# One load for the single-row B tiles of two batches, and a first load of 64 two-row descriptors, in a batched trace of a matrix product

## Chip, cores and metric

One core of a Trainium2 chip. The time is the device time of one execution in microseconds (us), as the median of several executions; lower is better. Engines go by their names in the profile: PE is TensorE, DVE is VectorE, ACT is ScalarE, POOL is GpSimd, SP is the sync engine. A descriptor orders one piece of a transfer and shows as one packet in the DMA records. A completion is the 4-byte packet with which each of the 16 DMA engines ends a load.

## The reference, cut to what matters

```python
B, N = 8, 2176
a, b: float32 [8, 2176, 2176]
prod = np.matmul(a, b)
traces = np.diagonal(prod, axis1=1, axis2=2).sum(axis=-1)     # float32 [8]
```

The trace of A·B needs no product: it is the sum over all elements of A transposed times B. The kernel has to read both inputs once, 303 MB of float32.

## The kernel before

A is loaded with a cast to bfloat16, transposed on TensorE and copied from PSUM into `at`; B is loaded with the same cast; DVE multiplies the two and sums. The loads go out from GpSimd, in one order. Per batch, A comes in groups of 6, 6 and 5 rows per partition, B in groups of 6, 6, 4 and 1. This is about the group with 1 and about the very first load, which must not wait for GpSimd and is therefore issued on the sync engine, without a cast.

```python
even = [6, 6, 4, 1]
UNEVEN = ((0, 64), (64, 116), (116, 123), (123, P))
...
single = ctx.enter_context(tc.tile_pool(name="single", bufs=3))
...
def fetch(t, src, start, m, parts=((0, P),)):
    rows = src[start:start + P * m, :].rearrange("(p r) k -> p r k", r=m)
    for lo, hi in parts:                       # usually one part, all 128 partitions
        with in_order():
            issued = nc.gpsimd.dma_start(out=t[lo:hi], in_=rows[lo:hi])
        loaded.append(issued)
    return t
...
def load_first(src, start):                    # 128 rows of A, one per partition
    words = stage.tile([P, MOST, N], bf16, tag="stage")
    plain = words.bitcast(f32).rearrange("p r k -> p (r k)")[:, :N]
    half = N // 2
    t = single.tile([P, 1, N], bf16, tag="single")
    nc.sync.dma_start(out=plain, in_=src[start:start + P, :])
    nc.scalar.copy(out=t[:, 0, :half], in_=plain[:, :half])
    nc.vector.tensor_copy(out=t[:, 0, half:], in_=plain[:, half:])
    return t
...
if not last:
    for start, m in b_groups:
        parts = UNEVEN if bi == BATCH // 2 and m == 1 else ((0, P),)
        on_dve(start // P, load(b[bi], start, m, parts))
```

`UNEVEN` cuts one single-row load into pieces whose sizes are no multiples of 16, so that the 16 DMA engines get different amounts. That is a means to balance them. The transposes of the first group and the end of the last batch are in the whole kernel.

## Time and profile before

| | before |
|---|---|
| median time | 709.01 us (708.89 to 709.24, 6 runs) |
| span of the profiled run | 707.4 us |
| share of the 16 DMA engines' span on GpSimd's queue | 99.8% |

The page and the chain are read in the prediction below. Three lines of the timeline at the start and one at the end are wanted later. The columns are start, duration, engine, line, operation, tiles; in brackets the idle time before and what ended it (SPq is the sync engine's issue of a DMA).

```profile
0.74 0.40 SPq L90 DMA_DIRECT2D words<-in_a_dram  x1
...
5.89 1.10 ACT L91 CAST t<-words 128x1088 bf16<-128x1088 f32 x1 [3.87 <-DMA words<-in_a_dram]
5.89 0.73 DVE L92 CAST t<-words 128x1088 bf16<-128x1088 f32 x1 [5.02 <-DMA words<-in_a_dram]
...
703.97 0.42 DVE L125 CUSTOM_DVE_ANT_0 at<-at,b_t 128x256 bf16<-128x256 bf16 x1 [0.24 <-DMA b_t<-in_b_dram]
```

The first load is used at 5.89 us, and the last piece of B at 703.97 us.

### The profile page before, as it was taken

The page shows a single profiled execution, that of the slowest core. Times are in us where ns is not written, and L with a number is a line of the kernel's source. Part 1 is how long each engine was busy: PE and PEld are TensorE (multiplying, and loading weights), DVE is VectorE, ACT ScalarE, POOL GpSimd, SP SyncE. Part 2 cuts the span into 40 slices and gives each one's busy share as a digit, 9 for nine tenths or more (in the row PEclk, how much of TensorE's full clock was granted, in tenths as well). Part 3 has the DMA queues.
Part 4 walks back from the last instruction along what each step waited for, and adds up shares of the span by engine and source line. Part 5 has one row for each costly group of instructions (what it writes and reads, how often), then busy time and mean ns, then how long its engine had stood idle before and what let it go on. Part 6 is the DMA issues. An engine that isn't in the chain of part 4 may idle for free.

```text
span 707.4 us, 3226 instructions
## 1 busy us (share of the span) xinstructions
PE 206.9 (29%) x1313; PEld 191.4 (27%) x1313; DVE 390.4 (55%) x132; ACT 202.8 (29%) x165; POOL 35.1 (5%) x72
## 2 busy tenths in 40 slices
PE   2452005700067000670016600156002660025504
PEld 1452005600066000560016500156002550025403
DVE  0216981359813597235972369623696227962397
ACT  2363005710057100570005800057001570016600
POOL 1000000000000000000000100000000000000200
PEclk9766556865567655785557955588555685557855
DMA  9999999999999999999999999999999999999997
GB/s 232 217 212 214 208 231 206 217 230 199 221 222 217 216 223 214 215 218 218 214 214 214 222 217 217 214 217 220 214 220 216 217 220 215 213 217 215 214 217 154
DMA packets 9025, 152.29 MB, mean 215 GB/s; under 512 B 1074, under 2 KB 1330, under 8 KB 2610
## 3 DMA queue, kind: packets, MB, share of 16 engines
q0 software_dynamic: 8864, 150.97, 99.8%
q1 hardware_dynamic: 146, 1.11, 0.5%
q8 instruction: 10, 0.16, 0.1%
q14 instruction: 5, 0.04, 0.0%
HBM read 303.04 MB, written 0.00 MB: 428 GB/s over the span
## 4 chain that ended last, share of the span: by engine, by line
DMA 56%; another core or an unknown queue 22%; issue 9%; PE 6%; ACT 3%; DVE 3%; POOL 1%; POOLq 0%; DVEq 0%; ACTq 0%
DMA t<-in_a_dram 30%; DMA t<-in_b_dram 21%; PE ps L148 6%; DMA b_t<-in_b_dram 5%; ACT at L120 3%; DVE at L125 2%; DVE at L118 1%; PE ps L172 0%; POOL t L73 0%; POOL b_t L255 0%; POOL shared L73 0%; POOL identity masks.py:199 0%; POOL identity masks.py:197 0%; DVE diagonal L125 0%
## 5 line engine op out<-in xcount | busy, mean ns | idle before, releaser
L120 ACT COPY at<-ps 128x1536 bf16<-128x1536 bf16 (+6 forms) x163 | 200.4, 1311 | 461.7 <-PE ps L148 445.5
L148 PE MATMUL ps<-identity,t 128*128 128x128 f32 x1071 | 187.4, 346 | 464.9 <-DMA t<-in_a_dram 443.5
L125 DVE CUSTOM_DVE_ANT_0 at<-at,t 128x13056 bf16<-128x13056 bf16 (+2 forms) x28 | 273.1, 9790 | 59.1 <-DMA t<-in_b_dram 59.1
L148 PEld LDWEIGHTS ps<-identity,t 128*128 128x128 f32 x1071 | 174.9, 212 | 476.5 <-issue 446.9
L118 DVE COPY at<-ps 128x1536 bf16<-128x1536 bf16 (+4 forms) x54 | 85.1, 1575 | 242.5 <-PE ps L148 213.0
L125 DVE CUSTOM_DVE_ANT_0 at<-at,shared 128x8704 bf16<-128x8704 bf16 (+3 forms) x5 | 29.2, 5838 | 5.8 <-DMA shared<-in_b_dram 5.8
L73 POOL DMA_DIRECT2D t<-in_b_dram x31 | 16.3, 531 | 264.9 <-PE ps L172 209.8
L73 POOL DMA_DIRECT2D t<-in_a_dram x24 | 13.0, 540 | 322.7 <-DVE sums L125 246.9
L265 PEld LDWEIGHTS <-at 128*128 128x128 bf16 x68 | 6.4, 132 | 30.6 <-issue 30.1
L172 PE MATMUL ps<-identity,t 128*128 128x128 bf16 x170 | 13.8, 219 | 2.9 <-ACT at L120 2.4
L265 PE MATMUL trace_ps<-shared,at 128*128 128x128 bf16 x59 | 5.9, 284 | 28.7 <-DMA shared<-in_b_dram 28.7
L172 PEld LDWEIGHTS <-t 128*128 128x128 bf16 x170 | 11.8, 99 | 5.4 <-issue 5.3
L73 POOL DMA_DIRECT2D shared<-in_b_dram x6 | 3.2, 532 | 47.3 <-PE ps L172 38.7
L92 DVE CAST t<-words 128x1088 bf16<-128x1088 f32 x1 | 0.7, 728 | 5.0 <-DMA words<-in_a_dram 5.0
L125 DVE DVE_READ_ACCUMULATOR2_ANT sums<- 128x1 f32 x28 | 2.3, 83 | 0.0
L91 ACT CAST t<-words 128x1088 bf16<-128x1088 f32 x1 | 1.1, 1098 | 3.9 <-DMA words<-in_a_dram 3.9
L265 PE MATMUL trace_ps<-b_t,at 128*128 128x128 bf16 x9 | 1.4, 296 | 1.1 <-DMA b_t<-in_b_dram 1.1
L255 POOL DMA_DIRECT2D b_t<-in_b_dram x3 | 1.6, 546 | 0.9 <-DMA shared<-in_b_dram 0.9
L125 DVE CUSTOM_DVE_ANT_0 at<-at,b_t 128x256 bf16<-128x256 bf16 (+1 forms) x3 | 1.5, 514 | 0.3 <-DMA b_t<-in_b_dram 0.2
L91 ACT ACT_TABLE_LOAD x1 | 1.3, 1283 | 0.7 <-PEq L307 0.7
L125 DVE DVE_READ_ACCUMULATOR2_ANT late<- 128x1 f32 x9 | 0.7, 82 | 0.0
L273 DVE TENSOR_REDUCE result<-total 1x7 f32<-1x28 f32 x1 | 0.2, 174 | 1.0 <-PE total L272 1.0
(13 smaller groups left out, 2.5 us busy)
## 6 DMA issues: line engine op xcount, KB each, us to landing
t<-in_a_dram POOLq DMA_DIRECT2D x16, 3264.0 KB, 45.1
t<-in_b_dram POOLq DMA_DIRECT2D x14, 3264.0 KB, 49.0
t<-in_a_dram POOLq DMA_DIRECT2D x7, 2720.0 KB, 42.4
t<-in_b_dram POOLq DMA_DIRECT2D x7, 2176.0 KB, 44.0
shared<-in_b_dram POOLq DMA_DIRECT2D x3, 2176.0 KB, 38.9
t<-in_b_dram POOLq DMA_DIRECT2D x6, 544.0 KB, 46.0
t<-in_a_dram POOLq DMA_DIRECT2D x1, 2176.0 KB, 14.9
words<-in_a_dram SPq DMA_DIRECT2D x1, 1088.0 KB, 5.1
```

The costliest lines, as they stand in the source:

```text
L73: issued = nc.gpsimd.dma_start(out=t[lo:hi], in_=rows[lo:hi])
L91: nc.scalar.copy(out=t[:, 0, :half], in_=plain[:, :half])
L92: nc.vector.tensor_copy(out=t[:, 0, half:], in_=plain[:, half:])
L118: last_copy = nc.vector.tensor_copy(out=dst, in_=src)
L120: nc.scalar.copy(out=dst, in_=src)
L125: nc.vector.tensor_tensor_reduce(out=x if out is None else out, in0=x, in1=y, scale=1.0, scalar=0.0, op0=MUL, op1=ADD, accum_out=acc,)
L148: nc.tensor.transpose(ps[:, n * m + r, :], words[:, r, c0:c0 + step * (P - 1) + 1:step], tiles[f32],)
L172: last_transpose = nc.tensor.transpose(ps16[:, n, r, :], a_t[:, r, c0:c0 + P], tiles[bf16],)
L255: loaded.append(nc.gpsimd.dma_start(out=row[:, lo:hi], in_=b[bi, start:start + P, lo:hi]))
L265: nc.tensor.matmul(trace_ps, x, y, start=(n == 0), stop=(n == len(pe_work) - 1),)
L273: nc.vector.reduce_sum(out=result[:1, 0:done], in_=total[:, 0:early].rearrange("o (b n) -> o b n", n=per_batch), axis=mybir.AxisListType.X,)
```

## The change

The intent is to save descriptors and completions in a kernel that only the DMA engines hold up: three loads for six single-row tiles of B, and 64 descriptors of two neighbouring rows (17,408 bytes) for the first load where there were 128 of one. The pieces move to the pair of batches 2 and 3. The diff, cut to its core (left out: the transposes for a tile with 64 partitions, and the renaming that splits `fetch` from the row pattern):

```diff
-    UNEVEN = ((0, 64), (64, 116), (116, 123), (123, P))
+    UNEVEN = ((0, 96), (96, 122), (122, P))
+    UNEVEN_BATCH = 2
...
-    single = ctx.enter_context(tc.tile_pool(name="single", bufs=3))
+    single = ctx.enter_context(tc.tile_pool(name="single", bufs=1))
+    pair_pool = ctx.enter_context(tc.tile_pool(name="pair", bufs=1))
...
-        plain = words.bitcast(f32).rearrange("p r k -> p (r k)")[:, :N]
-        t = single.tile([P, 1, N], bf16, tag="single")
-        nc.sync.dma_start(out=plain, in_=src[start:start + P, :])
-        nc.scalar.copy(out=t[:, 0, :half], in_=plain[:, :half])
-        nc.vector.tensor_copy(out=t[:, 0, half:], in_=plain[:, half:])
+        plain = words.bitcast(f32).rearrange("p r k -> p (r k)")[:, :2 * N]
+        t = pair_pool.tile([P, 2, N], bf16, tag="pair")
+        flat = t.rearrange("p r k -> p (r k)")
+        nc.sync.dma_start(
+            out=plain[32:96, :], in_=src[start:start + P, :].rearrange("(p r) k -> p (r k)", r=2)
+        )
+        nc.scalar.copy(out=flat[0:32, :], in_=plain[32:64, :])
+        nc.vector.tensor_copy(out=flat[32:64, :], in_=plain[64:96, :])
+        return t[0:64]
...
-                parts = UNEVEN if bi == BATCH // 2 and m == 1 else ((0, P),)
-                on_dve(start // P, load(b[bi], start, m, parts))
+                if m > 1 or bi == BATCH - 2:
+                    on_dve(start // P, load(b[bi], start, m))
+                    continue
+                if bi % 2 == 0:
+                    pair = pair_pool.tile([P, 2, N], bf16, tag="pair")
+                    both = b[bi:bi + 2, start:start + P, :].rearrange("b p k -> p b k")
+                    fetch(pair, both, UNEVEN if bi == UNEVEN_BATCH else ((0, P),))
+                on_dve(start // P, pair[:, bi % 2:bi % 2 + 1, :])
```

## The prediction

> **What bounds the kernel now.** I read the engine table and the slices of the page first, because they say which resource is never idle.
>
> ```profile
> PE 206.9 (29%) x1313; PEld 191.4 (27%) x1313; DVE 390.4 (55%) x132; ACT 202.8 (29%) x165; POOL 35.1 (5%) x72
> ...
> DMA  9999999999999999999999999999999999999997
> ```
>
> No compute engine is busy over 55% of the span, while the DMA row is 9 in every slice but the last. The queue part of the page says whose work that is.
>
> ```profile
> DMA packets 9025, 152.29 MB, mean 215 GB/s; under 512 B 1074, under 2 KB 1330, under 8 KB 2610
> q0 software_dynamic: 8864, 150.97, 99.8%
> q1 hardware_dynamic: 146, 1.11, 0.5%
> ...
> HBM read 303.04 MB, written 0.00 MB: 428 GB/s over the span
> ```
>
> The queue that GpSimd fills (loads with a cast from f32 to bf16) occupies the 16 DMA engines for 99.8% of the span. Only the first load, which has no cast, is on q1. Next, the chain of work in order of time, for the depth of the queue:
>
> ```profile
> 78.72 14.17 issue
> 92.89 0.01 POOLq L73
> 92.91 42.48 DMA t<-in_a_dram
> ...
> 670.56 33.38 DMA b_t<-in_b_dram
> 703.95 0.02 issue
> 703.97 0.42 DVE at L125
> ```
>
> A load issued at 92.91 us lands 42.48 us later, although its own data needs only some 13 to 15 us. The rest, about 28 us, is the wait behind earlier loads. So an issue that comes a few us late costs nothing. At the other end only 1.3 us of work (705.25 less 703.95) follow the last landing.
>
> The DMA records of the trace give the cost model. A 26,112-byte packet lasts 1942 ns, one of 17,408 bytes 1302 ns, one of 4352 bytes 342 ns; sizes are counted on the written side. All fit bytes / 13.6 B per ns plus 22 ns. Packets of one engine overlap by about 18 ns, so the start-to-start distance is bytes / 13.6 plus about 3.5 ns. A completion packet between two transfers adds about 21 ns. Per whole load with 6 rows this gives 8 x 1923.5 + 21 = 15,409 ns; completions of successive such loads stand 15,408 ns apart. The model is exact enough to count nanoseconds.
>
> **What the Trainium skill says.** All four are in "DMA: Bandwidth & Descriptors". (1) Section "Where 436 GB/s comes from" gives a port ceiling of 435.2 GB/s for the 16 engines. Our 13.6 B/ns written is 27.2 B/ns read, or 435 GB/s over 16 engines, and 428 GB/s are seen over the span. So the transfers are at the ceiling, and only overhead and unevenness remain. (2) Section "Why a DMA increments its semaphore by 16 and not by 1": some direct copies through GpSimd put ceil(partitions / 16) partitions on each engine in turn. The trace agrees: in the four-part load of batch 4, packet counts per engine are 10 on five engines, 9 on two, 8 on six, 4 on three. That is 4 each, plus 4 on engines 0 to 12 (52 partitions), plus 1 on engines 0 to 6 (7), plus 1 on engines 0 to 4 (5). The numbers 0 to 15 are my reading by that rule; the trace shows the counts. (3) Section "The descriptor swizzle": four neighbouring partitions belong to one engine, with a step from one half of the engines to the other at partition 64. Partitions 32 to 95 then give each engine four partitions, hence 4 packets of 17,408 bytes. No run so far shows this. (4) Section "Queues, rings and completion order" has an engine drain a packet of several descriptors from one ring before it changes rings. This agrees with the start: on each engine the first GpSimd packet begins only after the 8 packets of the first load (earliest completion 5.007 us, next packet 5.013 us).
>
> **The change, part by part.**
>
> *B tiles with one row, batches 0 to 5.* Removed: six loads of 544 KB, of which the one of batch 4 was in four pieces. Added: three loads of 1088 KB, of which the one of batches 2 and 3 is in three pieces. Batch 6 keeps a load of its own. The bytes are the same. The source rows of two batches are far apart, and the built instruction has the shape 128 x 2 x 2176, so I expect 256 packets of 4352 bytes per whole pair: no fewer packets. Completions: before, six whole singles (6 x 21 = 126 ns) and some 91 ns for the four pieces (a 9-packet engine took 3002 ns where 9 x 323.5 is 2911), in all 217 ns. After: two whole pairs and one single (63 ns) and three pieces, about 70 ns: 133 ns. Saving 0.08 us on every engine. Should the packets become 8704 bytes, 24 packets per engine fall away, and 24 x 3.5 = 0.08 us more.
>
> *First load.* Same 1.11 MB, at 8704 B in 328 ns per packet; 4 packets of 640 + 4 instead of 8 of 320 + 4 save 0.015 us of pure transfer. The beginning is less sure. The engines start between 1.76 and 2.65 us, most first packets last about 1 us (up to 1.43) and nearly all end near 3.0 to 3.3. Half as many descriptors might bring the late starters forward. I put 0.1 to 0.2 us on that.
>
> *Casts of the first load.* Each now has 32 partitions x 4352 elements instead of 128 x 1088. ACT took 1.10 us for 1088, so about 4.4 us for four times the length; DVE 0.73 us, so about 2.9 us. They end near 10 us instead of 7. Then come 16 f32 and 2 bf16 transposes with 64 rows and nine small copies, some 4 us, before the next A tile lands (its transposes began at 16.16 us). The B load that waits for this buffer is issued near 10 us instead of 7.28, and it lies behind loads that run until 46 us. Off the path: 0.
>
> *Buffers.* Single tiles go from three buffers to one, with one pair buffer beside it. The pair of batches 2 and 3 must wait for DVE's last product of batch 1; in the queue it stands behind all six other loads of batch 2, several of which need buffers freed no earlier. Batch 7's pieces wait for batch 6's product, near 630 us, and were issued at 668.6. Off the path: 0. Odd batches have one load less, so the 28 us of depth varies by 2.6 us (8 x 323.5), far from empty.
>
> *Balance of the engines.* The end is the slowest engine, not the mean. Ten instruction fetches of 16 KB (892 to 975 ns each) put whichever engine they fall on about 1.1 us behind. Comparing the 16 completion times of each load, I get the lag against the earliest engine near the end: 0, 1043, then thirteen between 1193 and 2351, and 2542 ns for the last. Mean about 1860, so the last engine is 0.68 us past it. The new pieces 96, 26 and 6, two rows each, put 18 packets on engines 0 to 5, 16 on 6 to 12, 12 on 13 to 15, where even is 16. Before, against an even 8: +2 on engines 0 to 4, +1 on 5 and 6, 0 on 7 to 12, -4 on 13 to 15. The only difference is engine 5 (+1, or 323 ns later) and engine 6 (-1, 323 ns earlier). Those two now hold the lags 2236 and 2542. If 6 is the later one, the maximum goes from 2542 to about 2560; if 5 is, to about 2865. So 0 to +0.32 us, with the start offsets (0 to 0.53 us) reshuffled by the new first load on top. I take +0.05, since whoever changed the pieces probably moved work the right way.
>
> Sum: -0.08 - 0.015 - 0.15 + 0.05 = -0.2 us, and with half a chance of merged packets -0.04 more: about -0.25 us.
>
> **The rivals.** First, balance dominates: a different first load and fetches falling elsewhere could put a lagging engine on +2 packets and the end 0.3 to 0.6 us later, 709.3 to 709.6. The 1.1 us per fetch speaks for it; against it, the pieces are nearly the same as before. Second, the queue runs dry: the pair buffer or the late casts delay an issue so far that DMA idles. It would cost whole microseconds, 711 or more, but 28 us of depth against a 3 us delay speaks against it. Third, the two-run pattern moves slower than one run. Half the rate on the three pairs, 3 x 5.2 us of transfer, would add up to 15 us and give 724; but rows of 8704 source bytes already moved at the ceiling as singles. Fourth, a better balance than I can work out: at most the 0.68 us above the mean, which gives about 708.
>
> **Range and chances.** From 709.0 us less 0.25 I predict 708.7 us. The range 707.9 to 709.4 covers a balance gain of most of the 0.68 us with the start's 0.2, and the bad balance of the first rival. 2% are 14 us; there is nothing of that size outside the third rival, so within 2% has 0.98.
>
> **What would show it.** DMA stays at 9 in all slices and GpSimd's queue near 99.8%; 256 packets per pair show as unchanged counts of 4352-byte packets (1152), a smaller count as merging. The first GpSimd packet starts near 4.9 us instead of 5.01. The first casts take about 4.4 and 2.9 us and nothing at 16 us moves. The completions of the last load show the balance. Wrong would be: a 0 to 8 in the DMA row, DVE or PE waiting on a load of pairs for many us, or a pair that takes clearly more than 5.2 us of the queue.

## The result, and the profile after

The changed kernel takes 709.37 us (median of 6 runs, 709.32 to 709.47) beside 709.01 us. The ratio is 1.0005, with a 95% interval from 0.9992 to 1.0018. It is the mean time of the one kernel's runs over that of the other's from the same rounds, so not quite the ratio of these medians. Its interval holds 1. Yet the lowest of the six is above the highest of the six before, so I take the 0.36 us as real and look for it. 708.7 was predicted, with a range to 709.4: inside, at the edge, and with the wrong sign.

From the page of the changed kernel, the DMA row of the slices and the queues:

```profile
DMA  9999999999999999999999999999999999999997
...
DMA packets 8897, 152.29 MB, mean 215 GB/s; under 512 B 1010, under 2 KB 1266, under 8 KB 2546
...
q0 software_dynamic: 8800, 150.97, 99.8%
q1 hardware_dynamic: 82, 1.11, 0.5%
```

The queue is as full as before. It has 64 packets fewer on q0 and 64 fewer on q1. On q1 those are the halved descriptors. On q0 they are completions: four sets of 16. The records still hold 1152 packets of 4352 bytes, so the pairs' rows did not merge. Now the start and the end of the timeline:

```profile
0.74 0.58 SPq L97 DMA_DIRECT2D words<-in_a_dram  x1
...
6.35 3.82 ACT L100 CAST t<-words 32x4352 bf16<-32x4352 f32 x1 [4.33 <-DMA words<-in_a_dram]
6.35 2.42 DVE L101 CAST t<-words 32x4352 bf16<-32x4352 f32 x1 [5.48 <-DMA words<-in_a_dram]
...
704.33 0.42 DVE L134 CUSTOM_DVE_ANT_0 at<-at,b_t 128x256 bf16<-128x256 bf16 x1 [0.19 <-DMA b_t<-in_b_dram]
```

The first load was issued in 0.58 us instead of 0.40 and is used 0.46 us later; the last piece of B is used 0.36 us later (704.33 less 703.97).

To split this, I take three numbers from the DMA records of each trace, over the 16 completions that each load leaves:

- S: their mean for the first load on GpSimd's queue (where the stream begins);
- M: their mean for the third four-row load of the last batch, at about 690 us (the work of the mean engine);
- L: how far the last of the 16 is behind that mean (the balance).

S + (M - S) + L is when the last engine finishes that load; from there to the end all engines still have the same work. In us:

| | S | M - S | L | last completion packet |
|---|---|---|---|---|
| before | 15.593 | 674.204 | 0.684 | 703.570 |
| changed | 15.729 | 674.122 | 1.025 | 703.965 |
| difference | +0.136 | -0.082 | +0.341 | +0.395 |

The three terms add up to the whole. The saving in completions is there, and it is the smallest of the three. After the last completion the changed kernel wins 0.15 us back: 0.06 up to the packet that carries the output (703.57 to 706.02 us before, 703.97 to 706.35 after), and 0.09 from there to the end of the span (1.34 us before, 1.26 after). So the two spans differ by 0.25 us, and so do the two traced executions, 709.38 and 709.13 us. That of before was one of its slower ones, hence 0.36 us between the medians. It is one traced execution each; how far S and L vary shows in the experiments.

### The profile page after: what moved, and what is told of

It reads as the page before. It is cut to its first block, busy times and chain, and to the rows that moved or that the text cites. A ratio compares the mean times of both kernels' runs of the same rounds, so it can differ in the third digit from the quotient of the medians.

```text
span 707.6 us, 3245 instructions
## 1 busy us (share of the span) xinstructions
PE 209.3 (30%) x1322; PEld 193.7 (27%) x1322; DVE 393.7 (56%) x134; ACT 204.3 (29%) x170; POOL 33.6 (5%) x68
## 3 DMA queue, kind: packets, MB, share of 16 engines
q0 software_dynamic: 8800, 150.97, 99.8%
## 4 chain that ended last, share of the span: by engine, by line
DMA 77%; issue 9%; PE 4%; another core or an unknown queue 3%; ACT 3%; DVE 2%; POOL 1%; POOLq 0%; DVEq 0%; ACTq 0%
DMA t<-in_a_dram 51%; DMA t<-in_b_dram 21%; DMA b_t<-in_b_dram 5%; PE ps L158 3%; ACT at L129 3%; DVE at L134 2%; PE ps L175 0%; DVE at L127 0%; POOL t L73 0%; POOL b_t L265 0%; POOL shared L73 0%; POOL identity masks.py:199 0%; POOL identity masks.py:197 0%; DVE diagonal L134 0%
## 5 line engine op out<-in xcount | busy, mean ns | idle before, releaser
L158 PE MATMUL ps<-identity,t 128*128 128x128 f32 (+1 forms) x1079 | 189.3, 347 | 463.1 <-DMA t<-in_a_dram 439.1
L158 PEld LDWEIGHTS ps<-identity,t 128*128 128x128 f32 (+1 forms) x1079 | 176.5, 212 | 474.8 <-issue 449.9
L134 DVE CUSTOM_DVE_ANT_0 at<-at,t 128x13056 bf16<-128x13056 bf16 (+2 forms) x22 | 259.0, 11799 | 61.6 <-DMA t<-in_b_dram 61.6
L127 DVE COPY at<-ps 128x1536 bf16<-128x1536 bf16 (+6 forms) x56 | 86.7, 1548 | 239.6 <-PE ps L158 223.5
L73 POOL DMA_DIRECT2D t<-in_b_dram x22 | 11.6, 529 | 264.9 <-PE ps L175 206.6
L175 PE MATMUL ps<-identity,t 128*128 128x128 bf16 (+1 forms) x171 | 13.6, 219 | 3.7 <-ACT at L129 3.6
L134 DVE CUSTOM_DVE_ANT_0 at<-at,pair 128x2176 bf16<-128x2176 bf16 x6 | 14.5, 2420 | 0.0
L175 PEld LDWEIGHTS <-t 128*128 128x128 bf16 (+1 forms) x171 | 11.9, 99 | 6.0 <-issue 5.8
L100 ACT CAST t<-words 32x4352 bf16<-32x4352 f32 x1 | 3.8, 3817 | 4.3 <-DMA words<-in_a_dram 4.3
L73 POOL DMA_DIRECT2D pair<-in_b_dram x5 | 3.2, 652 | 0.0
```

What stands on the lines that cost most here:

```text
L73: loaded.append(nc.gpsimd.dma_start(out=t[lo:hi], in_=rows[lo:hi]))
L100: nc.scalar.copy(out=flat[0:32, :], in_=plain[32:64, :])
L127: last_copy = nc.vector.tensor_copy(out=dst, in_=src)
L134: nc.vector.tensor_tensor_reduce(out=x if out is None else out, in0=x, in1=y, scale=1.0, scalar=0.0, op0=MUL, op1=ADD, accum_out=acc,)
L158: nc.tensor.transpose(ps[:, n * m + r, 0:high], words[:, r, c0:c0 + step * (P - 1) + 1:step], tiles[f32][0:high, 0:high],)
L175: last_transpose = nc.tensor.transpose(ps16[:, n, r, :], a_t[:, r, c0:c0 + P], tiles[bf16][0:high, 0:high],)
```

## The experiments

Theory A after this reading: the first load starts later, the completions save 0.08 us, and the new pieces balance the engines worse. Theory B: the first load with its longer casts costs everything, and the pairs are free. Four runs take the change apart. Each run had 5 rounds, and three groups of four runs each shared their runs of the kernel before: 708.96, 708.98 and 708.97 us (each group on another chip). The numbers of all traces stand together first:

| kernel | median us | traced us | first packet | S | M - S | L | last completion |
|---|---|---|---|---|---|---|---|
| before | 709.01 | 709.13 | 1.76 | 15.59 | 674.20 | 0.68 | 703.57 |
| changed | 709.37 | 709.38 | 2.11 | 15.73 | 674.12 | 1.03 | 703.97 |
| first load alone | 709.72 | 709.69 | 2.12 | 15.86 | 674.18 | 0.60 | 703.73 |
| pairs alone | 709.18 | 709.10 | 1.77 | 15.41 | 674.15 | 0.90 | 703.55 |
| six partitions as plain loads | 709.65 | 709.48 | 2.11 | 15.83 | 674.14 | 0.78 | 703.83 |
| whole pairs | 710.14 | 710.11 | 2.11 | 15.84 | 674.10 | 1.65 | 704.67 |
| old first load, old pieces, whole pairs | 708.95 | 708.75 | 1.75 | 15.42 | 674.17 | 0.49 | 703.18 |
| first load into partitions 0 to 63 | 710.99 | 711.20 | 2.07 | 17.45 | 674.09 | 1.13 | 705.77 |
| first load as 128 packets | 709.54 | 709.54 | 2.18 | 15.77 | 674.13 | 1.12 | 704.11 |
| first load alone, fills on GpSimd | 709.53 | 709.49 | 2.11 | 15.70 | 674.19 | 0.54 | 703.64 |
| first load alone, fills on DVE | 709.42 | 709.36 | 2.10 | 15.80 | 674.21 | 0.71 | 703.81 |
| first load in two halves | 710.03 | 709.66 | 2.05 | 16.24 | 674.17 | 0.64 | 704.13 |
| pairs alone, six as plain loads | 709.22 | 708.90 | 1.75 | 15.43 | 674.21 | 0.73 | 703.47 |
| pieces of 64, 56, 5 and 3 | 709.69 | 709.67 | 1.76 | 15.44 | 674.15 | 1.48 | 704.15 |

From the output's packet to the end of the span the five kernels without pairs need 1.34 to 1.40 us, the nine with pairs 1.21 to 1.26 us: those with pairs end some 0.13 us sooner after everything is computed. Why is not in the records. Not all of them keep it. The traced time is 1.75 to 1.80 us longer than the span in eleven kernels, but 1.92 to 1.94 us in three of those with the old first load and pairs (the pairs alone; old first load, old pieces, whole pairs; pieces of 64, 56, 5 and 3).

### The first load alone

```diff
 # changed kernel
-    if m > 1 or bi == BATCH - 2: ...          # pairs, pieces 96, 26, 6
+    parts = UNEVEN if bi == BATCH // 2 and m == 1 else ((0, P),)     # as before: 64, 52, 7, 5
+    on_dve(start // P, load(b[bi], start, m, parts))
```

> The changed first load alone, single B tiles as before. Theory A (three terms: later start +0.14 us on the mean engine, fewer completions -0.08 us, worse balance of the engines +0.34 us, the last from the new pieces): the start term is here, the other two are not. First load of six-row... that is, the first GpSimd load completes on the mean engine near 15.73 us (before 15.59), the latest engine is about 0.5 us past the mean near the end instead of 0.68, and the time is 708.9 to 709.1 us. Theory B (the first load, with its longer casts, costs the whole 0.36 us): 709.4 us.

709.72 us (709.69 to 709.83), more than either theory had. S and L are as theory A said in direction (15.86; L 0.60). But the time is 0.76 us above before, and the last completion packet, at 703.73 us, only 0.16 us later than before's. The rest is behind it:

```profile
703.50 0.27 PE L267 MATMUL trace_ps<-b_t,at 128*128 128x128 bf16 x2 [0.24 <-DMA b_t<-in_b_dram]
...
704.53 0.43 DVE L133 CUSTOM_DVE_ANT_0 at<-at,b_t 128x256 bf16<-128x256 bf16 x1 [0.62 <-DMA b_t<-in_b_dram]
```

The last piece is used 0.80 us after that packet began, before it was 0.40. In the records an 8 KB instruction fetch starts at 702.99 us, among the last pieces, and one of the last completion packets lasts 104 ns instead of 22. I made that a theory of its own, below.

### The pairs alone

```diff
 # kernel before
-                parts = UNEVEN if bi == BATCH // 2 and m == 1 else ((0, P),)
-                on_dve(start // P, load(b[bi], start, m, parts))
+                ...                            # the pairs and the pieces 96, 26, 6 of the change
```

> The pairs alone, with their pieces 96, 26 and 6 and one buffer, first load as before. Theory A: mean engine 0.08 us earlier near the end than before, but the two engines that get two instruction fetches each have only two packets less than even instead of four less, so the latest engine is some 0.9 us past the mean (before 0.68): 709.1 us. Theory B: 708.9 us.

709.18 us (709.08 to 709.30), with L = 0.90: theory A's 709.1, and 0.3 us more than theory B's. So the pairs with their pieces cost something without the new first load, though the mean engine has less to do (M - S is 0.05 us shorter).

### The pieces: six partitions as plain loads

```diff
 # changed kernel, batch 2
-                    fetch(pair, both, UNEVEN)
+                    fetch(pair, both, UNEVEN[:2])
+                    for s in range(2):
+                        fetch(pair[:, s, :], both[:, s, :], UNEVEN[2:])
```

> The changed kernel, but the last six partitions of the pair in pieces as two plain loads of one run each. Theory A with the rule that a plain load spreads from engine 0 and a two-run load goes on from where the last one ended: the six now fall on engines 0 to 5, the three highest engines get 12 packets instead of 14, the two engines with two fetches come out near 1.30 and 1.38 us on the scale where they are at 1.95 and 2.03, and the latest is another engine at 1.46 to 1.80; time 709.1 us (0.2 to 0.5 less than the changed kernel). If the spread does not depend on the shape: 709.4 us, lags as in the changed kernel.

The balance did what was expected. From the 16 completion times of the load before and the load after the pieces, the number of 4352-byte packets of every engine can be counted. In the changed kernel it is 18 on three engines, 16 on ten, 14 on three: the 26 partitions went to 13 engines, and the six went on from there, over the three last engines and the first three. Here it is 18 on six, 16 on seven, 12 on three: the two plain loads began again at the first engine. (Each fits to 10 ns over all 16 engines, the other count to 88 ns at best.) L fell from 1.03 to 0.78, and the last completion packet came at 703.83 us, 0.13 us before that of the changed kernel. The time did not follow: 709.65 us (709.48 to 709.76). In the traced run, the fastest of the five, this is at the very end:

```profile
704.75 0.29 DVE L134 CUSTOM_DVE_ANT_0 diagonal<-identity,trace_ps 128x128 bf16<-128x128 f32 x1
705.17 0.08 DVE L134 DVE_READ_ACCUMULATOR2_ANT late<- 128x1 f32 x1
```

The read of the sum comes 0.42 us after the product began; in the four traces around it that is 0.21 or 0.22. What held it back by 0.2 us is not in the records that I have. So the count of packets is shown, and the gain of 0.2 to 0.5 us in time that I expected from it is missed.

### Whole pairs

```diff
-                    fetch(pair, both, UNEVEN if bi == UNEVEN_BATCH else ((0, P),))
+                    fetch(pair, both)
```

> The changed kernel with all three pairs whole, every engine 16 packets. Theory A: the two engines with two fetches each lag 1.58 and 1.66 us past the mean near the end instead of 0.94 and 1.03, time 710.0 us. Theory B, or any in which the pieces do not matter: 709.4 us or a little less, for two completions fewer.

710.14 us (710.02 to 710.18), and two engines lag 1.53 and 1.65 us: theory A's number, and the largest single lesson on balance. Without pieces the kernel is 0.77 us slower. The two engines are those that get two of the ten 16 KB instruction fetches: in the records of before, the fetches at 44.5 and 641.3 us put the same engine behind, those at 127.5 and 669.6 us another, each by some 1.1 us. The other six fall on six different engines.

### Old first load, old pieces, whole pairs

```diff
 # pairs alone
+    UNEVEN = ((0, 64), (64, 116), (116, 123), (123, P))      # on batch 6's own load
-                    for lo, hi in UNEVEN if bi == UNEVEN_BATCH else ((0, P),):
-                        ...
+                    loaded.append(nc.gpsimd.dma_start(out=pair, in_=both))
```

> The first load as before, the three pairs whole, and the four pieces 64, 52, 7 and 5 of the kernel before put on the load that batch 6 keeps for itself. Balance theory: packets per engine stand to even exactly as before (+2 on engines 0 to 4, +1 on 5 and 6, -4 on 13 to 15), so the latest engine is again 0.6 to 0.7 us past the mean near the end, while completions are 0.06 us cheaper: 708.9 us, level with before and 0.2 to 0.3 less than the pairs with their own pieces (709.18). If pairs cost something by themselves: 709.2 us or more.

708.95 us (708.75 to 709.15), level with before (708.98 in the same rounds), 0.2 us under the pairs with their own pieces. L is 0.49. So whole pairs cost nothing that shows in the time; their own pieces did. This is the best version, and it does not beat the kernel before: the interval of the ratio, 0.9987 to 1.0012, lies around 1.

### The first load: where the late start comes from

All traces with 64 partitions in the first load have the first packet at 2.05 to 2.18 us, all with 128 at 1.75 to 1.77. Three runs tell what it is about the 64. First, other partitions:

```diff
-            out=plain[32:96, :], ...
+            out=plain[0:64, :], ...            # casts read 0 to 31 and 32 to 63
```

> The changed kernel with the first load put into partitions 0 to 63 instead of 32 to 95. If the late start comes from long packets or two-row runs: first packet again at 2.11 us (before 1.76), issue on the sync engine 0.58 us. If it comes from where the partitions lie: first packet near 1.76 us. Placement can also make the packets slower[...]: then the completions of the first load come later than the 5.45 us of the changed kernel, by up to 2.5 us, and the time is up to 2.5 us longer; else 709.4 us.

The first packet is again late (2.07 us), so where the partitions lie does not matter for that. It matters for everything after it:

```profile
0.74 0.54 SPq L97 DMA_DIRECT2D words<-in_a_dram  x1
...
9.04 3.82 ACT L100 CAST t<-words 32x4352 bf16<-32x4352 f32 x1 [7.02 <-DMA words<-in_a_dram]
```

The load is used at 9.04 us instead of 6.35, S is 1.7 us later and the time 710.99 us. Of the two placements, 32 to 95 is the better one. The records show how: the middle one of the 64 packets lasts 1367 ns instead of 655. All 16 engines carry the load in both placements, for 16 and more of its packets are under way at once, and no packet of GpSimd's queue begins before the load's first completions (6.82 us here, 5.18 us in the changed kernel). Next, short packets into the same 64 partitions:

```diff
-        plain = words...[:, :2 * N]
+        plain = words....rearrange("p (r k) -> p r k", r=2)[:, :, :N]      # a gap between the rows
-            out=plain[32:96, :], in_=....rearrange("(p r) k -> p (r k)", r=2)
+            out=plain[32:96], in_=....rearrange("(p r) k -> p r k", r=2)
```

> The changed kernel with the first load as 128 packets of one row, two for each of the partitions 32 to 95 (a gap between the rows keeps them apart). If long packets or two-row runs make the start late: first packet at 1.76 us, mean completion of the first GpSimd load near 15.5 to 15.6 us instead of 15.73 to 15.86, time 709.1 us. If 64 partitions from 32 on make it late: first packet at 2.11 us, 709.4 us.

The q1 queue has its 146 records back, and the first packet is later still, at 2.18 us; the issue takes longer too:

```profile
0.74 0.66 SPq L96 DMA_DIRECT2D words<-in_a_dram  x1
```

So long packets are not the cause. Last, 64 partitions with one row each, twice:

```diff
 # kernel before
-        nc.sync.dma_start(out=plain, in_=src[start:start + P, :])
+        for lo in (0, 64):
+            nc.sync.dma_start(out=plain[lo:lo + 64], in_=src[start + lo:start + lo + 64, :])
```

> The kernel before with its first load issued as two loads of 64 partitions, one row each (0 to 63, then 64 to 127). Looked at for the first packet: if 64 partitions by themselves make it late, it comes at 2.1 us; if two rows per partition do, near 1.75 us. [...]its packets should be slow and the first GpSimd load complete up to 1.7 us later: 709 to 710.7 us.

First packet at 2.05 us: 64 partitions by themselves make it late, with one row or two. (The time is 710.03 us. S is 0.65 us later than before, and the last packet of the second half ends at 12.19 us, where the one load of before was over at 5.52. What the rest of the time is was not looked for.) The mean of S is 15.46 us over the five traces with the old first load, and 15.79 us over the seven with 64 partitions from 32 on. The start therefore costs about 0.3 us, and the pair of traces that I compared first, with 0.14, had it small.

### The fetch at the end

The first load alone had lost 0.4 us after its last completion. Twelve fills on GpSimd, or 24 on DVE, do nothing but lengthen that engine's program and so move its later instruction fetches.

```diff
+        scratch = const.tile([P, 1], f32, tag="scratch")
+        for _ in range(12):
+            nc.gpsimd.memset(scratch, 0.0)
```

> The changed first load alone (709.72 us before), with twelve small fills on GpSimd in the first 100 us, which only move its later instruction fetches. Theory: the earlier run lost 0.35 us of its time because an 8 KB instruction fetch, at 702.99 us, fell among the last pieces of B and held the last landing back (0.8 us from last completion packet to use, instead of 0.4). With the fetch elsewhere the last landing is used within 0.4 us and the time is 709.3 to 709.4 us. If the fetch does not belong to GpSimd or is not the cause: 709.7 us again.

The miss: 709.53 us, a fetch still at 702.76 us, the last landing still used 0.68 us after its packet. Another fetch moved, from 329.8 to 257.1 us; that one is GpSimd's. The same on DVE:

```diff
+        for _ in range(24):
+            nc.vector.memset(scratch, 0.0)
```

> The changed first load alone, with 24 small fills on DVE before anything else there, to move DVE's later instruction fetches (the fills on GpSimd moved the fetch of 330 us to 257 us and left the one among the last pieces at 702.8 us, so that one is not GpSimd's). If it is DVE's, no 8 KB fetch falls between 702 and 704 us, the last landing is used some 0.4 us after the last completion packet instead of 0.7 to 0.8, and the time is 709.2 to 709.4 us. If not: 709.5 to 709.7 us again.

709.42 us (709.29 to 709.55). No fetch lies between 634 us and the last completion but those of 16 KB; the one of 702.99 us is now at 633.0, and another moved from 242 to 155 us. The end is as before:

```profile
704.19 0.42 DVE L136 CUSTOM_DVE_ANT_0 at<-at,b_t 128x256 bf16<-128x256 bf16 x1 [0.24 <-DMA b_t<-in_b_dram]
```

That is 0.38 us after the last completion packet at 703.81. So the fetch was DVE's, and it held the last landing back: 0.80 and 0.68 us in the two traces with it, 0.38 without. The gain in time is 0.3 us against the first load alone, but only 0.11 us against the fills on GpSimd, which kept the fetch (709.53). What is left in the traced executions, 0.23 us over before (709.36 and 709.13), is the late start (S +0.21) and L (+0.03). Between the medians it is 0.45 us (709.42 and 708.97), since the traced run of before lay above its median, with a late S.

### Two tries at a better balance

The first puts the two plain loads on the old first load:

```diff
 # pairs alone, batch 2
+   moves = [(pair[lo:hi], both[lo:hi]) for lo, hi in UNEVEN[:2]]
+   moves += [(pair[122:, s, :], both[122:, s, :]) for s in range(2)]
```

> The pairs alone on the old first load (709.18 us), with the last six partitions of the pair in pieces as two plain loads. As it did on the new first load, this should take two packets from each of the three highest engines and cut the lag of the last engine by 0.2 to 0.3 us (from 0.90): 708.9 us. If the extra load brings something else, as the time of that run did: 709.2 to 709.4 us.

L fell from 0.90 to 0.73, the time did not: 709.22 us, with one run, the traced one, at 708.90 and four at 709.19 to 709.22. It is the second time that the two plain loads cost what the balance gave; in most runs something of about 0.3 us comes back that the one traced run does not have. That stays open. The second try uses the plain rule with other sizes:

```diff
 # old first load, whole pairs
-    UNEVEN = ((0, 64), (64, 116), (116, 123), (123, P))
+    UNEVEN = ((0, 64), (64, 120), (120, 125), (125, P))
```

> Old first load, whole pairs, batch 6's load in pieces of 64, 56, 5 and 3 partitions: packets against even +2 on engines 0 to 2, +1 on 3 and 4, 0 on 5 to 13, -4 on 14 and 15. If the one of the three highest engines that gets no instruction fetch is 13, this is the best balance so far, lag 0.4 to 0.5 us and 708.9 us; if a twice-fetched engine is 13, it comes out about 1.6 us past the mean, with 710.0 us.

The bad branch: 709.69 us, one engine 1.48 us past the mean at 690 us. A twice-fetched engine is the one that now gets full measure. The lag was foreseen at 1.6; the time stayed 0.3 us under the 710.0 expected.

## Why the prediction was right or wrong

**The bound, and what lies off the path: right.** DMA is at 9 in all slices but the last, and GpSimd's queue at 99.8%. The casts took 3.82 and 2.42 us (4.4 and 2.9 predicted), moved nothing at 16 us that mattered, and the single buffers never emptied the queue. The longer casts cost the stream nothing, so theory B is out: M - S is 674.18 to 674.21 us in the three kernels that have only the new first load, beside 674.20. Rivals two and three (queue dry, two-run rows slow) did not happen. One reading behind the bound goes too far. The 435.2 GB/s that the prediction cites are a ceiling of the ports of the on-chip memory, and what is written through them here is 13.6 B per ns on 16 engines, or 217.6 GB/s; only what is read comes to 435. That the ports hold the engines at this rate is not shown, and nothing in the sum rests on it.

**Completions, -0.08 us: right,** -0.082 in the two traces. No packets merged, as expected. Over all traces it is somewhat less: M - S averages 674.190 us in the five kernels with 66 completions per engine, 674.126 in the four with 62, and is 674.096 in the one with 58. That is 12 to 16 ns for a completion where the model has 21.

**First load, -0.165 us: wrong in sign.** The step that failed is "Half as many descriptors might bring the late starters forward". The first packet came 0.35 us later, as with every load of 64 partitions, whatever its packets. About half of that is the issue itself, 0.58 us instead of 0.40 (0.54 to 0.66 us against 0.38 to 0.40 over the single loads of all runs). The other half passes between the end of the issue and the first packet, 0.79 us instead of 0.62. The first packet on GpSimd's queue began at 5.18 us instead of 5.01, where 4.9 was predicted. The mean engine started 0.14 us later in this pair of traces and about 0.3 over all. Partitions 32 to 95 were a good choice, as partitions 0 to 63 showed, but not for the reason given: four packets for each engine. The map behind it is one for 128 partitions. With 64, partitions 0 to 63 too kept all 16 engines busy, and it was the packets that became slower.

**Balance, +0.05 us: wrong in size,** +0.34 measured. The step that failed is the count "18 packets on engines 0 to 5, 16 on 6 to 12, 12 on 13 to 15". I had seen the rule on plain loads with one run per partition, which start at engine 0, and carried it over to loads with two runs. Those go on from where the last one ended: three engines got 18, ten 16, three 14. The two engines with two instruction fetches were among the three, kept two packets more than I gave them, and ended 0.94 and 1.02 us past the mean. The run with plain loads put the predicted count in place and these two fell back. The first rival named the danger, for another reason.

The sum was -0.25 and became +0.36 in the medians (+0.40 up to the last completion). The range held because it had room for the bad balance of the first rival. That the result fell inside, 0.03 us from the end, owes nothing to the sum: it is luck.

**What the runs show of the two causes, and how far.** The late start is in all eight traces with a single load of 64 partitions, and in the one with two. That balance sets the time is clearest between the four kernels with the old first load and pairs: L of 0.49, 0.73, 0.90 and 1.48 us go with 708.95, 709.22, 709.18 and 709.69 us. But the parts do not add up. The first load without the fetch at the end costs 0.45 us and the pairs alone 0.22, together 0.67, where the change costs 0.36. The 0.16 us outside the span that the pairs alone have, and the change does not, is part of the gap. The rest, 0.15 us, is open.

**What the prediction did not have:** the 0.15 us won back after the last completion; it had counted 1.3 us of work there and looked for no change in it.

**Open:** why the first packet of a load of 64 partitions comes later; what takes back the gain of the two plain loads; why the program ends sooner with pairs. One trace per kernel also limits the terms: S varied by 0.18 us between traces with the same first load, and the medians of several kernels lie up to 0.4 us above their traced run.

## What to carry to other kernels

When the DMA queue is full from end to end, the time is the slowest engine's: start, own bytes, and every instruction fetch that lands on it. Count packets per engine from the completion times of two successive loads before trusting a rule for how pieces spread; the rule can change with the shape of the load. A saving of descriptors is worth nanoseconds each here (by the prediction's model 3.5 ns for a packet and 21 ns for a completion; 12 to 16 ns for a completion over all traces), and a change made for it can lose more in how the load is issued.

## What the Trainium skill lacked or had wrong

- "DMA: Bandwidth & Descriptors", section "Why a DMA increments its semaphore by 16 and not by 1", has both rules (spread by ceil(partitions / 16), and a cursor that goes on) and says that some direct copies follow the first, but not which. Here a load with one run per partition followed the first (packet counts 10, 9, 8 and 4 in the kernel before; 18, 16, 12 with plain tails), one with two runs per partition the second (18 x3, 16 x10, 14 x3).
- The same page has no cost for the number of partitions of a load from the sync engine: 128 partitions were issued in 0.38 to 0.40 us with the first packet at 1.75 to 1.77 us; 64 partitions in 0.54 to 0.66 us with the first packet at 2.05 to 2.18 us.
- The same page, "The descriptor swizzle", gives the map for 128 partitions. No page has a measured load into 64 partitions from 32 on (what 0 to 63 cost is in "SBUF — State Buffer"). Here, from issue to landing, a load takes 5.6 us into 32 to 95, 8.3 us into 0 to 63, and 5.1 us into all 128; all 16 engines carry it each time.
- "Runtime: NRT & Kernel Launch", section "Instruction fetch mechanics", calls the cost of crossing a 16 KiB boundary "mostly hidden". In this kernel, which the DMA engines bound, it is not: each of the ten fetches (0.89 to 0.98 us) put one DMA engine some 1.1 us behind. And besides the 16 KB fetches the trace has fetches of 8 KB on another queue, two of them moved by fills on DVE and one by fills on GpSimd.
